# Long convolution by a two-stage transform: filters and short convolutions as two streams, filter spectra turned through DRAM, second stage without a split

## The chip, the cores and the metric

The kernel runs on one core of one Trainium2 chip. The metric is the device time of one execution in microseconds. The kernel before takes 4048.68 us (median of three runs, 4048.43 to 4051.03). The profile that is read below is one execution of 4047.38 us, of which 4045.6 us are the span from the first to the last instruction.

## What is computed

The kernel is one layer of an encoder on 2048 positions of 1024 channels. It has a projection, then two mixers side by side (a recurrent one, RWKV-7, and a long convolution, Hyena), a gated merge, and a dense feed-forward block. The change lies in the Hyena mixer, 512 channels wide:

```python
def long_conv(z, h_fwd, h_bwd, d_skip):
    L = z.shape[1]; n = 2 * L
    zf = jnp.fft.rfft(z, n=n, axis=1)
    hf = jnp.fft.rfft(h_fwd, n=n, axis=0) + jnp.conj(jnp.fft.rfft(h_bwd, n=n, axis=0))
    y = jnp.fft.irfft(zf * hf[None], n=n, axis=1)[:, :L]
    return y + z * d_skip

def hyena_mixer(u, conv_w, conv_b, ..., skip):
    u = short_conv3(u, conv_w, conv_b)            # 3 taps along the positions
    v, x1, x2 = jnp.split(u, 3, axis=-1)
    h = hyena_filters(L, ...)                     # a small network times exp(-t * delta)
    z = x1 * long_conv(v, h[:, 0, 0], h[:, 0, 1], sk[0])
    z = x2 * long_conv(z, h[:, 1, 0], h[:, 1, 1], sk[1])
    return z
```

## The kernel before

The program runs its stages one after the other: the projection (to about 650 us), the recurrent mixer (to about 1654 us, called the chain below), the Hyena mixer (1654 to about 2190 us), the merge and the feed-forward block. Only the end of the chain and the Hyena mixer are changed.

**The Hyena mixer** works on four tiles c of 128 channels (`HT` = 4). The Fourier transform of 4096 points is done as two stages of small matrix products. The first stage of a signal is `fwd` (four steps of eight 64x128x128 matmuls, then a copy from PSUM to a buffer U). Between the stages two indices, position and channel, must change places within blocks of 32: `flip` does this with four `nc.vector.transpose` of 128x1024 on VectorE (L1213), from U to a buffer V. The second stage is `step3`, one step for each of eight groups q of four 128x128 blocks.

**A product** (`product`, called twice for each c) multiplies a signal's spectrum with a filter's. For each q it does the filter's second stage (`load`: four matmuls L1267, a copy H to SBUF by ScalarE L1273, and four small DMAs that write a copy Hs with the partition blocks exchanged, L1277), the signal's second stage (`step3`), two elementwise products A and B on VectorE (L1304, L1305), and one step later the first stage of the inverse (`back`, L1289 and L1290, and a copy to Q by ScalarE L1291). `load` runs two steps ahead. For q over 0 the signal's second stage runs on a split of V in a high and a low part in fp32r: a cast on ScalarE (L197), a subtraction on VectorE (L198), and three matmuls of 512 columns (L202, L203, L204) in the place of four matmuls of 128 columns in fp32. The filter's second stage and q = 0 are in fp32. After product 1 come `inverse`, a product with x1 (L1381), `fwd` again, flips, and product 2. The result of product 2 is inverted and multiplied with x2 in `finish`, which runs inside the next c.

**The filters** come from `filt(c, o)`, a generator of 16 pieces (eight of the matmuls L1193 with the exponential window on ScalarE L1192 and the window product on VectorE L1197; eight of the matmuls L1183 with the copy L1184 to U) that ends with a flip. `pull` runs pieces between the steps of a product: in product 1 about one for each q and the rest in a burst behind it, in product 2 up to four for each q until there are none left. The pieces of the first filter begin in the last two steps of the chain and go on between the last four parts of its output (`gated`, `channel_major`), one piece behind each.

**The short convolutions** are `short(ct, byrest)`: four blocks of 512 positions, each a load from DRAM to one of two buffers cu (L1156), one ScalarE operation (L1158) and two VectorE operations (L1159, L1164). All four are written where the result is needed: x1 at the start of c, z for c+1 and x2 ahead of product 2.

**What sets the order.** TensorE's order is the order of the program text in this part (`manual_schedule`). The other engines' instructions are ordered by a scheduler that weighs program order and priorities (`high_priority(offset=FIRST)` draws an instruction forward). Each engine then works through its list in that fixed order, so an instruction that waits holds up all that stand behind it. DMAs are issued by SyncE (SP) or ScalarE (ACT), each in its own order. The PSUM pool has two buffers for each tag: `pz` (second stage), `pq`, `pf`, `po`.

## Time and profile before

| what | value |
|---|---|
| profiled execution, and its span | 4047.38 us, 4045.6 us |
| mean granted TensorE clock | 0.978 |
| TensorE busy | 3847.6 us, 95% of the span |
| VectorE busy | 2418.9 us, 60% |
| ScalarE busy | 1489.7 us, 37% |
| TensorE busy from 1700 to 2200 us, per 100 us | 88.9, 87.7, 89.3, 90.2, 82.7 us |
| VectorE busy from 1700 to 2200 us, per 100 us | 80.6, 81.6, 85.7, 78.6, 71.7 us |
| DMA share from 1700 to 2200 us | 0.20 to 0.30 |

One execution is profiled; times are microseconds unless marked ns. PE is TensorE, DVE VectorE, ACT ScalarE, SP SyncE. `L1213` is a line of the kernel before. A row of groups names line, engine, operation, output <- inputs by the program's names, the shapes and the number of instructions, then busy time and the mean of one in ns, then the idle time of the engine just before them and what ended it. A row of a timeline names start, length, and in brackets the idle time ahead with its releaser. In a table by windows PEclk is the granted TensorE clock as a share of full speed.

### The profile page before, as it was taken

The numbers are of one execution on the slowest core, as the hardware profiler recorded it, in microseconds if no ns is written. First come the engines' busy times: TensorE is split into PE (matmuls) and PEld (weight loads), VectorE is DVE, ScalarE is ACT, GpSimd is POOL, SyncE is SP. The second block draws the span as 40 slices with busy tenths as digits, with TensorE's granted clock in tenths as the row PEclk, the third lists the DMA queues.
The fourth block names the chain that finished last, engine by engine and source line by source line (L and its number), as shares of the span: only waits on it lengthen the run. The fifth ranks groups of instructions, "written<-read, shape, count | busy, mean of one in ns | idle before, by whom it ended". The sixth has DMA issues, their size and how long they took to land. (4 is left out here: it accounts for less than half of the span.)

```text
span 4045.6 us, 64349 instructions
## 1 busy us (share of the span) xinstructions
PE 3847.6 (95%) x25872; PEld 3135.6 (78%) x25872; DVE 2418.9 (60%) x3823; ACT 1489.7 (37%) x2914; POOL 76.8 (2%) x107
## 2 busy tenths in 40 slices
PE   8999999899998999788897999999999999999998
PEld 6766557777776777788887999788888878888887
DVE  4456884565666665678877655544444474444444
ACT  3345662333335565756554323211111151111113
POOL 0000000000000000000000000000000000000000
PEclk9999999999999999899999999999999999999999
DMA  4566878676677666322224434511111132111111
GB/s 137 171 169 178 216 201 240 197 211 195 207 214 206 198 188 200 91 56 69 62 74 145 151 117 126 167 52 47 47 47 47 47 116 93 47 47 47 47 47 42
DMA packets 389185, 501.83 MB, mean 124 GB/s; under 512 B 134852, under 2 KB 270541, under 8 KB 388181
## 3 DMA queue, kind: packets, MB, share of 16 engines
q1 hardware_dynamic: 362775, 443.13, 36.8%
q10 hardware_dynamic: 20736, 37.80, 3.1%
q0 software_dynamic: 5376, 16.78, 1.4%
q8 instruction: 204, 3.34, 0.4%
q14 instruction: 94, 0.77, 0.1%
HBM read 352.74 MB, written 127.93 MB: 119 GB/s over the span
## 5 line engine op out<-in xcount | busy, mean ns | idle before, releaser
L202 PE MATMUL acc<-xh,wh 128*128 128x512 f32 x1376 | 584.9, 425 | 9.2 <-ACT xh L197 9.2
L203 PE MATMUL acc<-xl,wh 128*128 128x512 f32 x1376 | 553.8, 402 | 6.9 <-DVE xl L198 6.9
L204 PE MATMUL acc<-xh,wl 128*128 128x512 f32 x1376 | 552.7, 402 | 0.5 <-DVE wl L198 0.5
L1644 DVE TENSOR_TENSOR acc<-pd,acc 128x1024 f32<-128x1024 f32 x320 | 387.8, 1222 | 68.7 <-PE pd L204 63.5
L197 ACT CAST fwh<-raw 128x1024 fp32r<-128x1024 f32 x132 | 138.5, 1049 | 703.8 <-PE pg L203 486.1
L202 PEld LDWEIGHTS acc<-xh,wh 128*128 128x128 f32 x1376 | 263.9, 192 | 125.0 <-issue 48.4
L1672 DVE TENSOR_TENSOR h<-pu,sg 128x512 f32<-128x512 f32 x88 | 60.9, 692 | 492.1 <-PE pu L204 486.1
L203 PEld LDWEIGHTS acc<-xl,wh 128*128 128x128 f32 x1376 | 265.0, 193 | 70.0 <-DVE xl L198 9.9
L204 PEld LDWEIGHTS acc<-xh,wl 128*128 128x128 f32 x1376 | 264.4, 192 | 65.6 <-DVE wl L198 1.1
L202 PE MATMUL pd<-fwh,hh 128*128 128x512 f32 x704 | 275.8, 392 | 2.1 <-DVE acc L1642 1.7
L204 PE MATMUL pu<-fxh,fwl 128*128 128x512 f32 x704 | 277.5, 394 | 0.0
L204 PE MATMUL pg<-fxh,fwl 128*128 128x512 f32 x704 | 277.1, 394 | 0.0
L203 PE MATMUL pg<-fxl,fwh 128*128 128x512 f32 x704 | 276.1, 392 | 0.0
L202 PE MATMUL pg<-fxh,fwh 128*128 128x512 f32 x704 | 275.9, 392 | 0.2 <-DVE fxl L1559 0.2
L202 PE MATMUL pu<-fxh,fwh 128*128 128x512 f32 x704 | 275.4, 391 | 0.4 <-ACT fxh L1558 0.4
L203 PE MATMUL pu<-fxl,fwh 128*128 128x512 f32 x704 | 275.8, 392 | 0.0
L203 PE MATMUL pd<-fwl,hh 128*128 128x512 f32 x704 | 275.2, 391 | 0.0
L204 PE MATMUL pd<-fwh,hl 128*128 128x512 f32 x704 | 274.2, 389 | 0.0
L198 DVE TENSOR_TENSOR fwl<-raw,fwh 128x1024 fp32r<-128x1024 f32 x132 | 161.3, 1222 | 167.0 <-ACT fwh L197 163.1
L198 DVE TENSOR_TENSOR wl<-wraw,wh 128x512 fp32r<-128x512 f32 (+1 forms) x217 | 169.3, 791 | 149.4 <-ACT wh L197 132.3
L197 ACT CAST wh<-wraw 128x512 fp32r<-128x512 f32 (+1 forms) x217 | 151.0, 705 | 290.5 <-PE acc L203 248.9
L1213 DVE STREAM_TRANSPOSE V<-U 128x1024 f32<-128x1024 f32 x96 | 181.2, 1955 | 30.3 <-ACT U L1291 12.4
(299 smaller groups left out, 7569.9 us busy)
## 6 DMA issues: line engine op xcount, KB each, us to landing
wraw<-in_w_in SPq DMA_DIRECT2D x130, 512.0 KB, 4.4
ABp<-ABd SPq DMA_DIRECT2D x64, 512.0 KB, 4.7
raw<-in_fg SPq DMA_DIRECT2D x44, 512.0 KB, 3.5
raw<-in_fu SPq DMA_DIRECT2D x44, 512.0 KB, 3.4
raw<-in_fd SPq DMA_DIRECT2D x44, 512.0 KB, 3.4
ud<-ev ACTq DMA_DIRECT2D x84, 256.0 KB, 3.4
ABd<-AB SPq DMA_DIRECT2D x32, 512.0 KB, 4.6
gated<-ev SPq DMA_DIRECT2D x64, 256.0 KB, 3.0
```

The source lines that it names most:

```text
L197: nc.scalar.copy(hi, src)
L198: nc.vector.tensor_tensor(out=lo, in0=src, in1=hi.bitcast(F32), op=ALU.subtract)
L202: mm(ps, ah, bh, start=start, stop=False)
L203: mm(ps, ah, bl, start=False, stop=False)
L204: mm(ps, al, bh, start=False, stop=stop)
L1213: self.nc.vector.transpose(V[:, :, sl].rearrange("p j c -> p c j"), U[:, :, sl].rearrange("p n c -> p c n"))
L1644: tt(out=acc[t], in0=pf, in1=acc[t], op=ALU.add)
L1672: tt(out=h, in0=put, in1=sg, op=ALU.mult)
```

## The change

Four things are rewritten together.

1. **Second stage.** `parts` and the split go, with the split constant matrix `Ms`. `step3` runs in fp32 for the signal at every q, as for the filter.
2. **Filter flips.** A filter's spectrum isn't flipped on VectorE any more. Each piece of 128x512 is copied from PSUM to one of two spots in SBUF (the free half of cu0, or ring buffer 11) and stored from there by ScalarE's DMA queue to a tensor `Hd` in DRAM; `turned_filter` loads V with four DMAs of 32 partitions on SP's queue, with the two indices exchanged. U then holds signals only.
3. **Filters as one stream.** `filters()` is one generator for all eight filters, `upto(n)` runs it to its piece n. In the last steps of the chain five pieces stand where 4.0 us of them stood, and between its last four output parts 2, 6, 1 and 0 in the place of one each. In product 1 the pieces but nine are spread over q, and nine follow in a burst. Ahead of product 2 stand four pieces, and 12 are spread over its q. The window and its product share a buffer.
4. **Short convolutions as one stream.** `shorts()` yields after each block of 512 in the order z(0), x1(0), z(1), x1(1), x2(0), z(2) and so on, and issues the load of the next block ahead of the work on this one. Four blocks are spread over the q of product 1 and eight over those of product 2 (four in the last). The first two `load` of product 1, which stood ahead of `finish`, now stand behind it.

```diff
-    def short(self, ct, byrest):
+    def shorts(self):
...
+        cts = [0, HT]
+        for c in range(HT):
+            cts += [c + 1, HT + c + 1, 2 * HT + c] if c + 1 < HT else [2 * HT + c]
+        seq = [(ct, b) for ct in cts for b in range(NB)]
...
+        u = given(0)
+        for k, (ct, b) in enumerate(seq):
+            nxt = given(k + 1) if k + 1 < len(seq) else None
...
+            u = nxt
+            yield
...
+    def filters(self):
...
+                def spec(q, g):
...
+                    u = self.spots[q % 2].rearrange("p (a b) -> p a b", b=P)
+                    nc.scalar.copy(u, p)
+                    nc.scalar.dma_start(self.Hd[c, o, 4 * q:4 * q + 4].rearrange("n p c -> p n c"), u)
...
-        self.Vfs[c, o] = self.flip(U)
+    def upto(self, n):
+        while self.pieces < n and next(self.taps, 0) is None:
+            self.pieces += 1
...
+    def turned_filter(self, c, o):
+        self.upto(32 * c + 16 * o + 16)
+        V = self.hy.tile([P, 32, P], F32, name="V", tag="post", bufs=3)
+        for k in range(4):
+            self.nc.sync.dma_start(V[32 * k:32 * k + 32], self.Hd[c, o, :, 32 * k:32 * k + 32])
+        return V
...
-            def step3(hi, lo, q):
+            def step3(v, q):
                 p = ps.tile([P, 4, P], F32, name="pz", tag="pz")
-                if lo is not None:
-                    self.mm3(p.rearrange("p a b -> p (a b)"), Mh, Ml, hi.rearrange("p a b -> p (a b)"), lo.rearrange("p a b -> p (a b)"), True, True)
-                    return p
                 for j in range(4):
-                    mm(p[:, j], Mc[:, 0 if 4 * q + j == 0 else 3], hi[:, j], start=True, stop=True)
+                    mm(p[:, j], Mc[:, 0 if 4 * q + j == 0 else 3], v[:, 4 * q + j], start=True, stop=True)
                 return p
...
-            def product(Vf, Vz, Q, fill, share, tag, hs):
-                AB = {}
-                room = s.tile([P, 16, P], F32R, name="vh", tag=tag, bufs=1)
+            def product(Vf, Vz, Q, goal, convs):
+                AB, begin = {}, self.pieces
+                hs = {q: load(Vf, q) for q in range(2)}
...
-                    pull(fill, share if q < 7 else 0.0)
+                    self.upto(begin + (goal - begin) * min(q + 1, 7) // 7)
                     if q > 0:
                         back(q - 1)
+                    for _ in range(convs * (q + 1) // 8 - convs * q // 8):
+                        next(self.conv)
...
-                for part in (gated(2), channel_major(1), channel_major(0), gated(0)):
+                for part, k in ((gated(2), 2), (channel_major(1), 6), (channel_major(0), 1), (gated(0), 0)):
                     self.pull(part, 1e9)
-                    self.pull(taps, 0.8)
-                self.taps = taps
+                    self.pull(taps(k), 1e9)
...
                 for c in range(HT):
                     x = zt("x1")
-                    moves = turned(self.short(HT + c, True), x)
-                    Vf = self.Vfs.pop((c, 0))
-                    hs = {q: load(Vf, q) for q in range(2)}
+                    moves = turned(self.short(HT + c), x)
                     if post:
                         finish(*post)
                     pull(moves, 1e9)
-                    taps = self.filt(c, 1)
-                    Q = product(Vf, Vz, self.pre(c + 1), taps, 0.8, "z", hs)
-                    pull(taps, 20.0)
+                    more, at = c + 1 < HT, 32 * c + 32
+                    Q = product(Vf, Vz, self.pre(c + 1), at - 9, 4 if more else 0)
+                    self.upto(at)
+                    Vf = self.turned_filter(c, 1)
...
-                    x2 = self.short(2 * HT + c, False)
-                    pull(taps, 1e9)
-                    taps = self.filt(c + 1, 0) if more else iter(())
-                    Vf = self.Vfs.pop((c, 1))
-                    Q = product(Vf, Vz, self.pre(c), taps, 3.0, "x1", {q: load(Vf, q) for q in range(2)})
-                    pull(taps, 1e9)
-                    post = c, Q, x2
+                    self.upto(at + 4)
+                    Q = product(Vf, Vz, self.pre(c + 1), at + 16, 8 if more else 4)
+                    post = c, Q, self.short(2 * HT + c)
                     if more:
+                        Vf = self.turned_filter(c + 1, 0)
```

The lists of two engines show where the scheduler puts this. The first place is ScalarE at the start of product 2 of the second channel tile. `pfz` is the PSUM of the forward transform, `z<-ph` the copies of the next tile's turned signal, `rg<-pz` the copies H of the filter's second stage, `pg` and `pf` a filter's two halves, `cu_16310` and `cu_16334` the two buffers of the short convolutions. The list before:

```order
L1248 COPY U<-pfz 128x4x128 x8
L1235 COPY z<-ph 128x512 x4
L1273 COPY rg<-pz 128x512 x3
L197 CAST vh<-V 128x512 x2
L1192 ACTIVATE rg<-delta,k_c_tcol 128x128 x4
L1184 COPY U<-pf 128x512
```

and the list of the change at the same place:

```order
L1278 COPY U<-pfz 128x4x128 x5
L1265 COPY z<-ph 128x512 x4
L1164 ACTIVATE co<-cu_16310,k_conv_b,k_conv_w 128x512
L1164 ACTIVATE co<-cu_16334,k_conv_b,k_conv_w 128x512
L1201 COPY cu_16310<-pf 128x512
L1211 ACTIVATE rg<-delta,k_c_tcol 128x128
L1202 DMA Hd<-cu_16310 128x4x128
L1211 ACTIVATE rg<-delta,k_c_tcol 128x128 x3
L1164 ACTIVATE co<-cu_16310,k_conv_b,k_conv_w 128x512
L1164 ACTIVATE co<-cu_16334,k_conv_b,k_conv_w 128x512
L1289 COPY rg<-pz 128x512 x3
```

The three copies H, which stood right behind the copies of z, now stand behind four blocks of a short convolution (x2), the last two of which are loaded into buffers that the first two must first give back.

The second place is VectorE from `finish` to the first steps of product 1, in the third channel tile. `co<-pv` is the product with x2 that ends `finish`, `rg<-pz` the products A and B. The list before:

```order
L1213 STREAM_TRANSPOSE V<-U 128x32x32 x8
L1330 TENSOR_TENSOR co<-pv,co 128x8x64 x2
L198 TENSOR_TENSOR vh<-V,vh 128x512 x2
L1330 TENSOR_TENSOR co<-pv,co 128x8x64 x2
L1304 TENSOR_TENSOR rg<-pz,rg 128x512
L1305 TENSOR_TENSOR rg<-pz,rg 128x512
L1197 TENSOR_TENSOR rg<-pg,rg 128x512
L1164 SCALAR_TENSOR_TENSOR co<-cu_16309,k_conv_w,cv 128x16x32
```

and the list of the change:

```order
L1244 STREAM_TRANSPOSE V<-U 128x32x32 x8
L1346 TENSOR_TENSOR co<-pv,co 128x8x64 x4
L1170 SCALAR_TENSOR_TENSOR co<-cu_16310,k_conv_w,cv 128x16x32
L1170 SCALAR_TENSOR_TENSOR co<-cu_16334,k_conv_w,cv 128x16x32
L1153 MEMSET cu_16334 128x1
L1165 SCALAR_TENSOR_TENSOR cv<-cu_16310,k_conv_w,cv 128x512
L1318 TENSOR_TENSOR rg<-pz,rg 128x512
L1170 SCALAR_TENSOR_TENSOR co<-cu_16310,k_conv_w,cv 128x16x32
L1216 TENSOR_TENSOR rg<-pg,rg 128x512
L1151 MEMSET cu_16310 128x1
L1165 SCALAR_TENSOR_TENSOR cv<-cu_16334,k_conv_w,cv 128x512
L1319 TENSOR_TENSOR rg<-pz,rg 128x512
```

The first product A (L1318) now stands behind the end of two convolution blocks and the first operation of a third, and B (L1319) behind the first operation of a fourth; in the list before no convolution stood ahead of them.

More of the change, by code (lines that the diff above doesn't have):

```diff
@@ L939, in chain, with taps @@
             more, left = columns(), [5.16 * 88]
+            def taps(k):
+                for _ in range(k):
+                    self.upto(self.pieces + 1)
+                    yield 0.87
             LAST = N - 3
@@ L1038, in chain @@
                 self.fps = ps, "pg", 3
-                taps, pieces = iter(()), [1, 2, 3]
+                self.taps, pieces = self.filters(), [1, 2, 3]
                 self.rush = 0
@@ L1099, in open @@
         self.Gc = [self.wp.tile([P, 16, 64], F32, name="Gc", tag="wl", bufs=2) for k in range(2)]
[L1100 to L1101 removed]
+        self.turns = dict(w=0, A=0, B=0, H=0, Hs=0)
+        self.smalls, self.pieces = {}, 0
+        self.spots = [cu[:, 514:1026], self.ring(11)]
         self.tcol = self.load(self.fp, "c_tcol")
@@ L1107, in open @@
         self.taken(0)
-        self.cus = [cu, self.ring(13, 514)]
-        self.z0 = self.short(0, True)
+        self.cus = [cu, self.wp.tile([P, 514], F32, name="cu1", tag="ex")]
+        self.conv, self.convs = self.shorts(), {}
+        self.z0 = self.short(0)
         for k in range(2):
@@ L1203, in filt @@
-        spec(7, last)
-        yield 0.87
-        self.Vfs[c, o] = self.flip(U)
+        for c in range(HT):
+            for o in range(2):
+                fw4, delta, skip = self.smalls.pop((c, o))
+                if (c, o) != (HT - 1, 1):
+                    self.small(c + o, 1 - o)
+                def spec(q, g):
+                    ps, tag, bufs = self.fps
+                    p = ps.tile([P, 4, P], F32, name="pf", tag=tag, bufs=bufs)
+                    for j in range(4):
+                        mm(p[:, j], self.Fc[:, 4 * q + j], g[:, j], start=True, stop=True)
+                    u = self.spots[q % 2].rearrange("p (a b) -> p a b", b=P)
+                    nc.scalar.copy(u, p)
+                    nc.scalar.dma_start(self.Hd[c, o, 4 * q:4 * q + 4].rearrange("n p c -> p n c"), u)
+                last = None
+                for q in range(8):
+                    g = self.next("w")
+                    ps, tag, bufs = self.fps
+                    p = ps.tile([P, 4, P], F32, name="pg", tag=tag, bufs=bufs)
+                    for j in range(4):
+                        n = 4 * q + j
+                        nc.scalar.activation(g[:, j], delta, AF.Exp, scale=self.tcol[:, n:n + 1])
+                        mm(p[:, j], self.H3[:, n], fw4, start=True, stop=n != 0)
+                        if n == 0:
+                            mm(p[:, j], self.e0[0:1], skip[0:1], start=False, stop=True)
+                    with self.tc.high_priority(offset=2 * FIRST):
+                        nc.vector.tensor_tensor(out=g, in0=p, in1=g, op=ALU.mult)
+                    yield
+                    if q > 0:
+                        spec(q - 1, last)
+                        yield
+                    last = g
+                spec(7, last)
+                yield
```

106 lines of the change are left out of this document (28 added, 78 removed).

## The prediction, as put on record

> **What bounds the kernel now.** I read the shares of the engines first, then windows over the stage that changes, then who TensorE waits for there, then the timeline around the longest waits.
>
> ```profile
> PE 3847.6 (95%) x25872; PEld 3135.6 (78%) x25872; DVE 2418.9 (60%) x3823; ACT 1489.7 (37%) x2914; POOL 76.8 (2%) x107
> ...
> 1900.00:2000.00 100.00, 89.25 (x777) 83.18 (x775) 85.69 (x98) 57.95 (x119) 0.00 (x0) 0.98 0.26 70
> 2100.00:2200.00 100.00, 82.71 (x704) 76.81 (x703) 71.67 (x83) 41.87 (x81) 0.00 (x0) 0.95 0.30 85
> ```
>
> In the window rows the columns are PE, PEld, DVE, ACT and POOL busy, then the granted clock and the DMA share. TensorE bounds this stage too, but VectorE is nearly as full (85.7 of 100 us). What can be won is TensorE's idle time, some 10 us in 100. The waits from 1605 to 2200 us (total, times, longest):
>
> ```profile
> PE pz L1267 <- DVE V L1213: 15.5, 5, 6.0
> PE pgt L874 <- ACT y L866: 11.2, 8, 4.4
> PE pg L1193 <- DVE rg L1197: 9.3, 10, 2.2
> PE pv L1328 <- ACT rg L1336: 8.8, 4, 2.9
> PE pfz L1246 <- DVE z L1381: 8.3, 6, 1.5
> PE pz L202 <- DVE rg L1305: 4.7, 3, 1.6
> PE pf L1183 <- ACT U L1184: 2.3, 2, 1.2
> ```
>
> Most are waits for VectorE, and short ones. No one wait is the kernel's limit: the sum of many decides, and so where the change puts work on VectorE and ScalarE counts as much as how much it takes away.
>
> **Part 1, second stage without a split.**
>
> ```profile
> 1967.91 1.06 PE L1267 MATMUL pz<-V,Mc 128*128 128x128 f32 x8
> 1968.72 0.48 PE L202 MATMUL pz<-vh,Ms 128*128 128x512 f32 x1
> 1969.04 0.40 PE L203 MATMUL pz<-vh,Ms 128*128 128x512 f32 x1
> 1969.28 0.39 PE L204 MATMUL pz<-vh,Ms 128*128 128x512 f32 x1
> 1969.51 1.05 PE L1193 MATMUL pg<-fw,H3b 128*128 128x128 f32 x8
> 1970.40 0.39 PE L1289 MATMUL pq<-rg,Mc 128*128 128x128 f32 x2
> ```
>
> From start to start, an fp32 group and a split trio take 1969.51 - 1967.91 = 1.60 us, and a fp32 group of four takes 1970.40 - 1969.51 = 0.89, so two take 1.78. Seven q in eight products make 56 trios: 56 x 0.18 = **+10** on TensorE, all on the path.
>
> What goes elsewhere:
>
> ```profile
> L1213 DVE STREAM_TRANSPOSE V<-U 128x1024 f32<-128x1024 f32 x96 | 181.2, 1955 | 30.3 <-ACT U L1291 12.4 <-ACT U L1248 10.8 <-ACT U L1184 7.0
> L198 DVE TENSOR_TENSOR vh<-V,vh 128x512 fp32r<-128x512 f32 x56 | 38.1, 686 | 0.5 <-ACT vh L197 0.5
> L197 ACT CAST vh<-V 128x512 fp32r<-128x512 f32 x56 | 33.7, 616 | 30.1 <-DVE V L1213 22.9 <-PE pz L204 6.3
> ```
>
> VectorE loses 38.1 here and ScalarE 33.7.
>
> **Part 2, filter flips through DRAM.** 32 of the 96 transposes go, a third of 181.2, or 60 us; with the subtractions VectorE has about 98 us less to do. ScalarE gets 64 issues. The nearest rows for the transfers (KB each, then us from issue to landing):
>
> ```profile
> rg<-rg SPq DMA_DIRECT2D x256, 64.0 KB, 2.0
> cu<-ud SPq DMA_DIRECT2D x22, 256.5 KB, 3.2
> ...
> yrd<-yo SPq DMA_DIRECT2D x16, 256.0 KB, 2.9
> ...
> N<-Nd POOLq DMA_DIRECT2D x8, 512.0 KB, 5.0
> ```
>
> A store of 256 KB takes 2.9, four loads of 128 KB (512 KB in all) at most 5.0: with the last copy 0.6 a filter is back about 9 after its last piece. The shortest cover is at the change of c: four forward steps of two groups of 0.89 (7.1), and in `finish` eight groups of inverse and four of transposes; with the 16 transposes of x1 that is some 14 of TensorE's work (the smaller ones counted at 0.45 a group). I cost it at nothing; if that cover were gone it would be a wait at each of eight filters (a rival below). DMA is busy only 0.26 to 0.30 of the time.
>
> With those flips out of VectorE's list, three sorts of short waits should go: pfz for z 8.3, pz for L1305 4.7, pf for U 2.3, together **-15**. The bounds are 0 and that plus the 9.3 of pg for L1197; I take the middle row because the burst of nine pieces, where pg waits, stays.
>
> **Part 3, the filter stream.** At the end of the chain:
>
> ```profile
> 1643.76 0.36 PE L1193 MATMUL pg<-fw,H3b 128*128 128x128 f32 x1
> 1648.21 0.47 PE L874 MATMUL pgt<-k_c_ident,y 128*128 128x128 f32 x1 [4.08 <-ACT y L866]
> ...
> 1649.14 1.92 PE L1183 MATMUL pf<-rg,Fc 128*128 128x128 f32 x8
> ```
>
> Six pieces of 0.89 now stand ahead of this wait and fill the 4.08 (the 4.4 of the table of waits lies earlier and stays, since no piece is put there). The piece after it ran at half pace (1.92), so another 2 comes back: **-6**, with -4 more at the start of the mixer, where the first filter's pieces no longer alternate with VectorE: **-10**, bounds 0 and -14.
>
> **Part 4, the short convolutions.** Here I expect the loss. Rows for durations:
>
> ```profile
> L1164 DVE SCALAR_TENSOR_TENSOR co<-cu,k_conv_w,cv 128x512 f32<-128x512 f32 x29 | 31.4, 1117 | 0.3
> L1158 ACT ACTIVATE co<-cu,k_conv_b,k_conv_w 128x512 f32<-128x512 f32 x16 | 13.0, 813 | 10.8 <-DMA cu<-ud 10.8
> L1164 DVE SCALAR_TENSOR_TENSOR co<-cu,k_conv_w,co 128x512 f32<-128x512 f32 x16 | 12.0, 751 | 0.4
> L1159 DVE SCALAR_TENSOR_TENSOR co<-cu,k_conv_w,co 128x512 f32<-128x512 f32 x16 | 11.9, 747 | 5.9 <-ACT co L1158 5.7
> L1304 DVE TENSOR_TENSOR rg<-pz,rg 128x512 f32<-128x512 f32 x64 | 44.0, 688 | 43.5 <-PE pz L204 34.6 <-PE pz L1267 8.8
> L1273 ACT COPY rg<-pz 128x512 f32<-128x512 f32 x64 | 37.2, 585 | 28.3 <-PE pz L1267 21.3 <-DMA rg<-rg 4.5 <-DVE rg L1304 2.4
> ...
> SPq L1156 <- DVE co L1164: 45.0, 20, 10.0
> ```
>
> The last row says that a load of cu already waits for the VectorE operation that frees its buffer (20 times). What is queued behind it is the matter.
>
> *Start of product 2.* Before:
>
> ```profile
> 2006.64 7.40 DVE L1213 STREAM_TRANSPOSE V<-U 128x1024 f32<-128x1024 f32 x4 [3.71 <-ACT U L1248]
> ...
> 2008.78 2.33 PE L1267 MATMUL pz<-V,Mc 128*128 128x128 f32 x19
> 2014.18 1.13 PE L1267 MATMUL pz<-V,Mc 128*128 128x128 f32 x8 [3.07 <-DVE V L1213]
> ```
>
> TensorE waits 3.07 for the four flips of Vz. In the change, count from F, the end of the forward transform. VectorE: three flips (1.85 each) from F+0.7 to 6.3, two filter products (0.69, as L1304) to 7.6, the fourth flip to 9.5, then block 1 of x2 (0.75 + a filter product 0.69 + 0.75) to 11.7. Only then is cu0 free; its load lands at 14.9, ScalarE works on it to 15.7; cu1 is free at 13.2, lands at 16.4, is done at 17.2. Behind these two in ScalarE's list stand the copies H, so the first is there at 17.8. TensorE: 16 transposes of z and two pieces to F+4.1, a wait for the filter product to 7.0 (2.9), a piece each of pf and pg and two filter steps to about 10.5; the third step needs a PSUM buffer that the copy H frees: wait to 17.8 (**7.3**). A further 1.1 goes to B, whose exchanged copy takes the swap's 2.0 and its issues. Together 11.3 against 3.07, or +8.2 in c = 1 and 2. In c = 0 one block stands ahead in the place of two, so about +4: **+20** in all. Bounds: if the loads were there in time only the flips' wait is left, 0; if each block cost its full load once more, 30.
>
> *Start of product 1 in c = 1, 2, 3.* Count from T, the end of x1's transposes. They free the row buffer that two waiting blocks write; VectorE ends the first at T+1.1, the load lands at 4.3, ScalarE ends at 5.1, and copy H of the third group at 5.7, where TensorE, with five groups of 0.89, stood at 4.5 (wait 1.2). VectorE's A comes after this block, at 6.5, and B after 1.12 + 0.69 + 0.75 + 0.69 more, at 9.8, against TensorE at 6.6: wait 3.2. About 4.5 each, nothing of it before: **+13**; bounds 0 and 20.
>
> *`finish`.*
>
> ```profile
> 1943.11 1.15 PE L1328 MATMUL pv<-k_c_ident,rg 128*128 128x128 f32 x8 [2.87 <-ACT rg L1336]
> 1944.09 3.60 PE L1232 MATMUL ph<-k_c_ident,co 128*128 128x128 f32 x16
> ...
> 1944.00:1948.00 4.00, 4.00 (x24) 3.64 (x23) 2.61 (x3) 2.03 (x4) 0.00 (x0) 0.57 0.15 66
> ```
>
> The two filter steps ahead of it (1.78) are moved behind it, so that much cover is gone while VectorE does the same eight flips: the wait of 2.87 becomes about 5. Three times +2.2: **+7**, bounds 0 and +9.
>
> **The clock.** After that 2.87 us wait the granted clock stood at 0.57, and 16 transposes took 3.60. The longest wait of the stage shows the same:
>
> ```profile
> 2145.60 3.64 PE L1267 MATMUL pz<-V,Mc 128*128 128x128 f32 x16 [6.00 <-DVE V L1213]
> ```
>
> Two groups that take 1.78 took 3.64, so a long wait costs 1.9 more behind it. The wait of 7.3 does so three times (5.7), the 3.2 perhaps every second time (2.8): **+9**; bounds 0 and 15. The Trainium skill, TensorE: Matmul & The Clock Gate, Part 1, has a threshold: half the clock after an idle window of about 3.4 us, with a free-running window. By that rule alone only the 7.3 would pay, and the sum would be 3 us lower; the 2.87 with its 0.57 shows that here a shorter wait can pay too.
>
> **The sum.** 10 - 15 - 10 + 20 + 13 + 7 + 9 = +34 on the profiled 4047.4, so 4081. The profiled execution lies 1.3 below the median, within the runs' spread (4048.4 to 4051.0), so I say **4082**.
>
> **The rivals.**
> *Relief wins (faster).* One mechanism: VectorE, with 98 us less, is early at the start of product 2, so that blocks 1 and 2 of x2 are done while the forward transform still runs and the loads of blocks 3 and 4 are there when ScalarE comes to them. It decides there: the second block would have to be done on VectorE by F+6.5 (TensorE's 10.5 less 3.2 of load and 0.8 of ScalarE), where I have 13.2. Then the 20, 13 and 9 fall away: 4047.4 + 34 - 42 = 4039, and with half of pz's 15.5 for V gone too, 4032. For it: VectorE is 85.7% full, and all these waits are on it. Against it: VectorE's list puts the blocks behind three or four flips, which wait for the last forward copy and cannot be early.
> *Half and half.* The loads wait, but only for one block, as in c = 0: half of 20 + 13 + 9 falls away, 4082 - 21 = 4061; with pg's 9.3 gone as well, 4052: no change.
> *The trip through DRAM is the bound.* If stores and loads, behind SP's small swaps, took twice the 9, TensorE would wait 5 and lose 1.9 in clock at the four changes of c: 4082 + 28 = 4110. Against it: DMA is busy 0.26.
>
> **How the numbers follow.** 0.51 for the forecast, 0.30 for relief, 0.12 for half and half, 0.07 for DRAM. Changes under 0.2% (8 us) can't be told from none here. Faster: 0.30; same: most of half and half and no more, 0.11; slower: the rest, 0.59. The forecast's own range is 4057 (the four losses of 20, 13, 7 and 9 at half: 4081 - 24) to 4106 (at their upper bounds 30, 20, 9 and 15: 4081 + 25). For 8 in 10 the range has to take in relief, with some more of the waits for VectorE gone: 4022 to 4106.
>
> **What would show it.** Right: a wait of 6 to 8 us of pz for the copy H at the start of product 2 in c = 1 and 2, with ScalarE idle there for a load of cu; a wait of pz for a VectorE product some 5 us into product 1; VectorE's busy time about 100 lower; no PE wait for a V that comes by DMA; the wait of 4.08 for y gone and the one of 4.4 still there. Wrong: if waits at the start of product 2 stay near 3 us, the convolution blocks were not in the way, and the time is then below 4040.

## The result, and the profile after

The changed kernel takes 4107.41 us (median of four runs, 4103.74 to 4115.43) against 4049.47 us for the kernel before in the same session (four runs, 4048.43 to 4051.03). The ratio is 1.0145, with a 95% interval of 1.0128 to 1.0163: **58 us slower**. The forecast was 4082, slower; the result is 25 us above it and 1.4 above the upper end of the range.

The profiled execution took 4106.99 us (span 4105.2, mean granted clock 0.969). The page's first part:

```profile
PE 3884.3 (95%) x26152; PEld 3176.9 (77%) x26152; DVE 2346.5 (57%) x3734; ACT 1462.0 (36%) x2857; POOL 76.8 (2%) x107
```

and the same two windows of 100 us as before (columns PE, PEld, DVE, ACT, POOL busy, granted clock, DMA share, GB/s):

```profile
1900.00:2000.00 100.00, 86.79 (x710) 83.17 (x709) 56.46 (x68) 44.99 (x94) 0.00 (x0) 0.89 0.43 111
2100.00:2200.00 100.00, 81.23 (x703) 75.68 (x703) 65.77 (x64) 42.56 (x82) 0.00 (x0) 0.90 0.46 118
```

VectorE is relieved: 56.5 us busy in a window where it had 85.7. TensorE is idle only a little more (86.8 busy, before 89.3). The number to see is the granted clock: 0.89 and 0.90, where it stood at 0.98 and 0.95.

To say how much each is worth, I cut the stage into windows of 2 us, from the same wait of the chain (`pR`, at 1606 us before) to the last inverse's wait for its flips, and added up three things. Idle is the window less TensorE's busy time; work is busy time times granted clock; clock is busy time times what is missing of the clock.

| from one profiled execution each, us | length | idle | work | clock |
|---|---|---|---|---|
| kernel before | 575.3 | 79.3 | 471.8 | 24.2 |
| changed kernel | 634.2 | 98.2 | 480.9 | 55.1 |
| difference | +58.9 | +18.9 | +9.1 | +30.9 |

All of the loss lies in this stage, and **just over half of it is the clock** (30.9 of 58.9).

The waits of TensorE from 1605 to 2260 us in the changed kernel (total, times, longest):

```profile
PE pz L1283 <- ACT rg L1289: 27.4, 16, 5.8
PE pf L1199 <- DVE rg L1216: 15.5, 8, 2.9
PE po L1335 <- DVE V L1244: 9.8, 4, 3.7
PE pv L1344 <- DVE co L1346: 6.8, 6, 2.8
PE pz L1283 <- DMA V<-Hd: 6.8, 1, 6.8
PE pgt L875 <- ACT y L867: 6.7, 4, 5.7
PE ph L1262 <- ACT z L1265: 5.6, 4, 4.9
PE pg L1212 <- DVE rg L1216: 5.5, 5, 1.5
PE pf L1199 <- ACT rg L1201: 3.5, 1, 3.5
...
PE pfz L1276 <- DVE z L1392: 0.3, 1, 0.3
```

The longest group is new: pz waits for ScalarE's copy H (L1289). The waits of pfz for z, 8.3 before, are nearly gone. The start of product 2 in the third tile, on TensorE:

```profile
2048.09 2.08 PE L1199 MATMUL pf<-rg,Fc 128*128 128x128 f32 x8 [2.86 <-DVE rg L1216]
...
2051.43 1.95 PE L1283 MATMUL pz<-V,Mc 128*128 128x128 f32 x16
2059.18 3.78 PE L1283 MATMUL pz<-V,Mc 128*128 128x128 f32 x16 [5.80 <-ACT rg L1289]
```

and on ScalarE at the same time:

```profile
2055.98 0.81 ACT L1164 ACTIVATE co<-cu,k_conv_b,k_conv_w 128x512 f32<-128x512 f32 x1 [3.76 <-DMA cu<-ud]
2057.84 0.81 ACT L1164 ACTIVATE co<-cu,k_conv_b,k_conv_w 128x512 f32<-128x512 f32 x1 [1.05 <-DMA cu<-ud]
2058.56 1.05 ACT L1289 COPY rg<-pz 128x512 f32<-128x512 f32 x2
```

The copy H that TensorE waits for stands behind two convolution operations, and ScalarE sits idle for the load of each. TensorE's rows show what the wait does besides: sixteen matmuls of the filter's second stage take 1.95 ahead of it and 3.78 behind it.

`finish` in the same tile, on TensorE:

```profile
1960.11 3.68 PE L1335 MATMUL po<-V,Gc 128*64 128x128 f32 x32 [2.02 <-DVE V L1244]
...
1969.53 0.63 PE L1344 MATMUL pv<-k_c_ident,rg 128*128 128x128 f32 x4 [1.56 <-DVE co L1346]
```

and in windows of 3 us around the first of these waits:

```profile
1956.00:1959.00 3.00, 1.97 (x19) 1.59 (x17) 3.00 (x2) 2.03 (x4) 0.00 (x0) 1.00 0.84 169
1959.00:1962.00 3.00, 1.89 (x18) 1.89 (x20) 3.00 (x3) 0.00 (x0) 0.00 (x0) 0.50 0.03 5
1962.00:1965.00 3.00, 3.00 (x24) 2.34 (x22) 3.00 (x3) 1.17 (x2) 0.00 (x0) 0.50 0.00 0
```

A wait of 2.02 us, and the clock is at 0.50 for the next five.

The filters' way through DRAM, by the DMA issues of that window (KB each, median us to landing):

```profile
V<-Hd SPq DMA_DIRECT2D x32, 512.0 KB, 7.8
...
Hd<-cu ACTq DMA_DIRECT2D x32, 256.0 KB, 2.5
Hd<-rg ACTq DMA_DIRECT2D x32, 256.0 KB, 2.6
```

The loads of V are 512 KB each, four to a filter, not the 128 KB that I had read into them, and land after 7.8 us, not 5.0 at most. In the changed kernel that is seen once, in the last tile:

```profile
2195.17 7.66 PE L1283 MATMUL pz<-V,Mc 128*128 128x128 f32 x40 [6.80 <-DMA V<-Hd]
```

### The profile page after: what moved, and what is told of

Read it like the earlier page. It is cut to its first block, busy times and chain, and to the rows that moved or that the text cites. A ratio compares the mean times of both kernels' runs of the same rounds, so it can differ in the third digit from the quotient of the medians.

```text
span 4105.2 us, 64939 instructions
## 1 busy us (share of the span) xinstructions
PE 3884.3 (95%) x26152; PEld 3176.9 (77%) x26152; DVE 2346.5 (57%) x3734; ACT 1462.0 (36%) x2857; POOL 76.8 (2%) x107
## 3 DMA queue, kind: packets, MB, share of 16 engines
q1 hardware_dynamic: 364311, 459.91, 38.4%
## 5 line engine op out<-in xcount | busy, mean ns | idle before, releaser
L1283 PE MATMUL pz<-V,Mc 128*128 128x128 f32 x1024 | 142.9, 296 | 36.5 <-ACT rg L1289 27.4
```

What stands on the lines that cost most here:

```text
L1283: mm(p[:, j], Mc[:, 0 if 4 * q + j == 0 else 3], v[:, 4 * q + j], start=True, stop=True)
```

## The experiments

All ratios are to the kernel before on the same chip, where it took 4033 to 4038 us, with 95% intervals. One execution of each was profiled; it lies up to 18 us from the median of its runs, so differences of a few us in the stage are read only where a named wait shows them. Idle, work and clock are those of the stage as above. The theory is that of the prediction: the convolution's loads in ScalarE's list make the loss. Its rivals: TensorE's extra work, the trip through DRAM, and, once the result was seen, the clock.

**The change once more.**

> The change itself, beside the same runs of the kernel before as the three that follow, whose ratios are to be read against this one. All theories: a ratio of 1.013 to 1.0165.

1.0153 (1.0125 to 1.018). The stage has idle 101.4, work 481.1, clock 58.2: the same picture on another chip.

### One part alone

**Second stage unsplit, in the kernel before.**

```diff
-                if q == 0:
-                    return v, None
+                return v, None
...
```

> The kernel before with the second stage unsplit for the signal, and nothing else. Theory 'order': +10 us of TensorE work, less up to 10 us of waits for VectorE and ScalarE that have 38 and 34 us less to do: 4049 to 4062. Theory 'split': 4080 or more. 'DRAM': as 'order'.

1.0038 (1.0022 to 1.0054), +15 us. In the stage work is up 13, clock 10, idle down 2.6. VectorE and ScalarE lose 38 and 34 us of operations, and TensorE's idle time hardly moves. The term of +10 for TensorE's work held (9.1 in the change itself); that less work on VectorE gave so little idle time back is a first sign against the -15, though that term was for the flips.

**Filter flips through DRAM, in the kernel before** (stored from U, loads where the flip stood).

```diff
+            nc.scalar.dma_start(self.Hd[c, o, 4 * q:4 * q + 4].rearrange("n p c -> p n c"), U[:, 4 * q:4 * q + 4])
...
-        self.Vfs[c, o] = self.flip(U)
+        V = self.hy.tile([P, 32, P], F32, name="V", tag="post", bufs=3)
+        for k in range(4):
+            nc.sync.dma_start(V[32 * k:32 * k + 32], self.Hd[c, o, :, 32 * k:32 * k + 32])
+        self.Vfs[c, o] = V
```

> The kernel before with the filters' flips replaced by the trip through DRAM (store from U on ScalarE's queue, four loads on SP's), and nothing else. VectorE loses 60 us of flips. Theory 'order': waits for VectorE shrink by 5 to 15 us, 4034 to 4050. Theory 'DRAM': 4080 or more, with TensorE waiting for V that comes by DMA.

1.0109 (1.007 to 1.0149). Work 471.2, as before; idle 103.4 and clock 39.0. Its waits:

```profile
PE pz L1272 <- DMA V<-Hd: 23.3, 5, 9.0
PE pq L1295 <- DVE rg L1310: 19.8, 3, 6.8
PE pz L1272 <- ACT rg L1278: 18.3, 4, 6.5
```

The second row is not a VectorE wait at its root. Product B needs the swapped copy Hs, and SyncE issued its swaps behind the loads of V, on the same queue, and VectorE waits for them:

```profile
1766.64 2.63 SPq L1209 DMA_DIRECT2D V<-Hd  x4
1769.37 2.41 SPq L1282 DMA_DIRECT2D rg<-rg  x4
...
1779.95 0.69 DVE L1310 TENSOR_TENSOR rg<-pz,rg 128x512 f32<-128x512 f32 x1 [6.86 <-DMA rg<-rg]
```

The queue held the swaps up by the 2.6 us of these issues. The longer part of the wait is their landing: all were issued by 1771.8, and the last of them came at 1779.95, just behind the last load of V (1779.14), where a swap lands after 2.0 us in the kernel before. So the trip costs on its own, wherever nothing long enough stands in front of it. The changed kernel escapes these waits by putting the filter's first steps behind `finish`.

**The change with the split put back** in the signal's second stage.

```diff
...
-                    p = step3(Vz, q)
+                    p = step3(Vz, q, zs)
+                    if q < 7:
+                        zs = parts(Vz, q + 1, room)
...
```

> The change with the split second stage of the kernel before, and nothing else undone. If the unsplit stage costs its TensorE work alone: 10 us less than the change, ratio 1.012 to 1.0135. If it costs the 15 to 20 us that it cost alone on the kernel before: 1.0095 to 1.0115. If the casts and subtractions come in the way of the streams: 1.015 or more.

1.018 (1.0159 to 1.0201), not faster than the change. TensorE's work falls to 471.4 as it should, but idle rises to 112.6: the waits of pz for ScalarE's copy H grow from 27.4 to 29.1 + 7.3. The profiled execution is the slowest of its four, 15 us above their median, so these sizes are rough. They fit the third expectation, that the casts and subtractions push the copies back further; no row here singles it out.

### One placement undone

**The two first filter steps ahead of `finish` again.**

```diff
...
                     moves = turned(self.short(HT + c), x)
+                    hs = {q: load(Vf, q) for q in range(2)}
                     if post:
                         finish(*post)
...
```

> The change with the first two filter steps of product 1 ahead of finish, as before. Theory 'order': the waits of 2.0 us for the flip and of 1.4 to 2.8 us for the product with x2 shrink by some 2 us each time and the clock stays up behind them: 3 x (2 + 3) = 15 us at most, ratio 1.0105 to 1.013. Rival (the flips of VectorE set that wait, whatever stands ahead): 1.014 to 1.016.

1.0131 (1.0105 to 1.0157). The waits in `finish` fall from 9.8 to 3.7 for V and from 6.8 to 0.4 for the product with x2 that its transposes wait for, and those for the copy H fall from 27.4 to 19.0. Waits for V from DRAM come instead: 13.7 (2.6, 2.7 and 8.4; a fourth of 2.5 is put down to nothing), where the change has 6.8. Much of what `finish` gives comes back as the trip.

**The convolutions where they were**, all four blocks written where the result is needed; the load of the next block is still issued one block ahead.

```diff
-            cts += [c + 1, HT + c + 1, 2 * HT + c] if c + 1 < HT else [2 * HT + c]
+            cts += [c + 1, 2 * HT + c, HT + c + 1] if c + 1 < HT else [2 * HT + c]
...
-                    Q = product(Vf, Vz, self.pre(c + 1), at - 9, 4 if more else 0)
+                    Q = product(Vf, Vz, self.pre(c + 1), at - 9, 0)
...
+                    x2 = self.short(2 * HT + c)
                     self.upto(at + 4)
-                    Q = product(Vf, Vz, self.pre(c + 1), at + 16, 8 if more else 4)
-                    post = c, Q, self.short(2 * HT + c)
+                    Q = product(Vf, Vz, self.pre(c + 1), at + 16, 0)
+                    post = c, Q, x2
```

> The change with the short convolutions in the order and at the places of the kernel before (x2 whole ahead of product 2, none inside the products). Theory 'order': the waits of pz for the copy H at the start of product 2 (27 us in all) mostly go, with the clock behind them: 4107 - 20 to 35, ratio 1.006 to 1.0105. Rival (the blocks have to be done somewhere, and VectorE does them later in the way of something else): 1.0125 or more.

1.0131 (1.0108 to 1.0155), some 6 to 9 us less than the two runs of the change, whose intervals overlap with it. It doesn't take the wait at product 2 away:

```profile
PE pz L1283 <- ACT rg L1289: 22.1, 13, 4.5
PE pg L1212 <- DVE rg L1216: 11.2, 6, 3.5
PE pv L1344 <- DVE co L1346: 10.3, 5, 4.2
```

ScalarE at the start of product 2 in the third tile:

```profile
2041.65 0.81 ACT L1164 ACTIVATE cv<-cu,k_conv_b,k_conv_w 128x512 f32<-128x512 f32 x1 [3.39 <-DMA cu<-ud]
...
2043.76 1.05 ACT L1289 COPY rg<-pz 128x512 f32<-128x512 f32 x2
```

In the place of x2's last blocks, blocks of another convolution (by the text's order, x1 of the next tile) now stand ahead of the copies H and wait for their loads, and TensorE waits 4.50, 3.39 and 4.16 at the three starts. The waits of pg and pv grow. So it does not matter which convolution stands there; what hurts is that an operation that waits for a load stands ahead of the copies.

**The chain's end as before**, one piece between each of its last four parts.

```diff
-                for part, k in ((gated(2), 2), (channel_major(1), 6), (channel_major(0), 1), (gated(0), 0)):
+                for part, k in ((gated(2), 1), (channel_major(1), 1), (channel_major(0), 1), (gated(0), 1)):
```

> The change with one piece of the filters between the last parts of the chain's output, as before, in the place of 2, 6, 1 and 0; the rest of the first filter follows behind. Theory 'order': the pieces wait for each other's window products and spots there (3.5 us for a spot, then 4.9 us for z behind them) and gain nothing; without them 0 to 10 us come back. Rival (they fill the wait of 4 us for y, as I forecast): 4 to 10 us more.

1.0158 (1.0133 to 1.0182), the same as the change. Waits of 1.48 (pg), 3.75 (pgt for y) and 2.77 (pz for V from DRAM) stand in the place of 3.52 (pf for the first spot's copy) and 4.89 (ph for z).

### The order of the lists

**ScalarE in the order of the text**, as TensorE.

```diff
-            with tc.manual_schedule(engines={mybir.EngineType.PE}):
+            with tc.manual_schedule(engines={mybir.EngineType.PE, mybir.EngineType.Activation}):
```

> The change, with ScalarE's list in the order of the program text in the Hyena mixer (TensorE's is so already). The copies H then stand ahead of the short convolution's blocks at the start of product 2. Theory 'order' (the loss is made by waiting blocks of the short convolution in front of what TensorE needs, and by the clock that falls after each such wait): the waits of pz for the copy H of 3.5, 4.5 and 5.8 us go, and with each about 2 us of half clock: 4107 - 20, so 4080 to 4095. Theory 'split' (the unsplit second stage costs more than its 10 us) and theory 'DRAM' (the trip of the filters costs it): within 4 us of 4107.

The theory's strongest test: no work, no transfer and no place in TensorE's list changes, only the order of ScalarE's list, and with it what stands ahead of the copies H.

```profile
PE pfz L1276 <- ACT U L1278: 9.0, 2, 8.7
PE pr L203 <- DVE y L198: 7.8, 1, 7.8
...
PE pz L1283 <- ACT rg L1289: 6.1, 5, 2.5
...
PE pr L202 <- DVE rs L1453: 5.2, 1, 5.2
```

The waits for H fall from 27.4 to 6.1, and the stage up to the merge (its first matmul pr) from 624.5 to 599.2, where the kernel before has 566.7. Idle time falls by 8 of these 25 us (94.5 to 86.2) and the clock's loss by 18 (54.6 to 36.4): the order of ScalarE's list cost more in clock than in waiting. The time is 1.0133 (1.0101 to 1.0165) all the same, which can't be told from the change's 1.0145 and 1.0153. Text order is wrong at the two ends: a forward transform at the start waits 8.7 for a copy of U, and the merge behind the mixer waits 7.8 and 5.2.

**VectorE in the order of the text too.**

> As before, with VectorE's list in the order of the program text too: no block of a short convolution stands ahead of the products A and B any more; the fourth flip goes ahead of the window products. Theory 'order': the waits of 2.2 us at the start of product 1 go as well, 4070 to 4090. 'split' and 'DRAM': within 4 us of 4107.

1.0179 (1.0144 to 1.0214). One row has grown from 15.5:

```profile
PE pf L1199 <- DVE rg L1216: 40.7, 7, 6.7
```

In this order the window products stand behind all four flips of a signal.

### The clock

**Redundant matmuls where TensorE waits**, in the change (three groups ahead of the first pf of the four pieces at product 2, four to six behind its second filter step, two in `finish`) and in the kernel before (three groups ahead of the flipped steps, three among the transposes of `finish`). Their results are overwritten by the matmuls behind them, or are the same once more.

```diff
+            def warm(p, n):
+                for k in range(4 * n):
+                    mm(p[:, k % 4], Mc[:, 3], Mc[:, 3], start=True, stop=True)
...
```

> The change with redundant fp32 matmuls, whose results are overwritten or are the same, put where TensorE waits: three groups of four ahead of the first pf at the start of product 2, four or six ahead of its third filter step, two ahead of the inverse in finish. Some 11 groups or 10 us of added work for each channel tile, none of it needed. Theory 'idle clock' (the clock halves after waits of about 2 us and more, and 31 of the 59 us lost are that): the waits are filled, the clock stays up, and the time falls by 12 to 25 us, a ratio of 1.008 to 1.0115 to the kernel before. Theory 'load clock' (the clock falls because of the heavier fp32 work, not because of idling): no fall, or a rise by up to 20 us, 1.0145 to 1.020.

> The kernel before with redundant matmuls in its two long waits of each channel tile (three groups ahead of the signal's first step of product 2, six in the last; three ahead of the second transpose of finish). Theory 'idle clock': of 10 us lost to the clock between the first product 2 and the last inverse, 5 to 10 come back, ratio 0.9972 to 0.9990. Theory 'load clock': 1.000 to 1.003.

| us in the stage | idle | work | clock |
|---|---|---|---|
| change, its second run | 101.4 | 481.1 | 58.2 |
| change with redundant matmuls | 88.5 | 510.8 | 37.2 |
| before | 79.3 | 471.8 | 24.2 |
| before with redundant matmuls | 65.0 | 495.2 | 17.5 |

The clock comes back in both: 21 us of it against 30 of added work in the change, 7 against 23 before. So it is the waiting that takes the clock, and not more matmuls. No time comes of it: 1.0181 (1.0157 to 1.0206) and 1.0005 (0.9991 to 1.002). In the kernel before the stage even became 2 us longer: gaps that end when another engine's work ends are filled, but not shortened. The added work was also more than the waits took in: 30 us of it replaced 13 of idle time in the change, and 23 replaced 14 before. A smaller dose was not tried.

### Putting the better halves together

**Loads ahead of `finish`, one piece between the chain's parts, ScalarE in text order in the first three tiles only**; and the same with the split.

```diff
...
-                for c in range(HT):
+            for c in range(HT):
+                hand = {mybir.EngineType.PE, mybir.EngineType.Activation} if c + 1 < HT else {mybir.EngineType.PE}
+                with tc.manual_schedule(engines=hand):
...
```

> The change with three of its orders put right together: the first two filter steps of product 1 ahead of finish, one piece between the chain's last parts, and ScalarE in the order of the program text inside the first three channel tiles (copies H ahead of the short convolution; the end is left to the scheduler). Theory 'order': most of the loss is order, and with it put right 25 to 45 us come back: ratio 1.0035 to 1.0085. Rival (each cure only moves the wait to the next VectorE product): ratio 1.010 or more.

> The same three orders with the split second stage of the kernel before, so that the streams and the trip through DRAM are what is left of the change. TensorE has 10 us less work, VectorE 38 and ScalarE 34 more. If the unsplit stage costs only its TensorE work: 10 us below the run without the split. If it costs the 15 to 20 us that it cost alone, and VectorE's relief of 60 us is then worth something: at or below the kernel before, ratio 0.995 to 1.002. If the casts and subtractions come in the way: above the run without the split.

1.0103 (1.0075 to 1.0132) and **1.0069 (1.0045 to 1.0094)**, the best of all. The waits for H are gone from the first rows, and one stands in their place (each kernel has its row):

```profile
PE pz L1283 <- DMA V<-Hd: 26.6, 5, 6.4
```

```profile
PE pz L1296 <- DMA V<-Hd: 25.8, 5, 6.6
```

The trip is now in the open. In mix_split the last store of a filter was issued at 1772.9, the loads at 1777.7 to 1779.5, and TensorE went on at 1791.6: 19 us, where I had said 9.

The kernel of the second of these (mix_split) was executed once more, unchanged, on the chip of the next two versions.

> One look more at the run with the three orders put right and the split second stage, beside the two that follow: within 8 us of its 4064, with four waits of about 6 us for the filter from DRAM.

4071.83 us in this one execution, some 8 us more than there, with idle 88.8 and clock 38.4 against 87.1 and 35.9.

**Product 2's pieces over five q in the place of seven**, so that a filter ends two steps earlier, with the split and without (`n` is 5 in product 2 and 7 in product 1).

```diff
-                    self.upto(begin + (goal - begin) * min(q + 1, 7) // 7)
+                    self.upto(begin + (goal - begin) * min(q + 1, n) // n)
```

> The same kernel with the 12 pieces inside product 2 spread over its first five q in the place of seven, so that each filter starts its trip through DRAM some 10 us earlier. If the trip is the cause of what was left: the waits for the filter of about 6 us in c = 1, 2, 3 go and with them 15 to 25 us, ratio 1.000 to 1.003. If something else takes their place (the flips of Q, the product with x2): less than 8 us gained, ratio 1.005 or more.

> The same without the split. If the trip is the cause of what was left: 15 to 25 us below the 4079 of the mixed unsplit kernel, ratio 1.004 to 1.007. Its distance to the run with the split gives the price of the unsplit stage once more: 10 us by its work.

1.0112 (1.0095 to 1.0129) and 1.0099 (1.0083 to 1.0114). With the split, V is waited for 18.8 in the place of 25.8, but the denser pieces make new waits (pfz for U 7.5). Without it the waits for V did not shrink at all (28.2), though the stores were earlier. ScalarE and SyncE say why:

```profile
1771.44 0.37 ACTq L1202 DMA_DIRECT2D Hd<-rg  x1
...
1776.96 6.12 SPq L1154 DMA_DIRECT2D cu<-ud  x3
1783.17 2.00 SPq L1235 DMA_DIRECT2D V<-Hd  x4
...
1797.02 3.75 PE L1283 MATMUL pz<-V,Mc 128*128 128x128 f32 x16 [6.59 <-DMA V<-Hd]
```

The last store went at 1771.44, and the loads of V stood on SyncE's queue until 1783.17, behind loads of cu that wait for their buffers. A late convolution holds up the filter. The price of the unsplit stage, 15 us alone and 15 between the two mixed versions, does not show here: the version without the split is 10 us shorter than the one with it (4073.76 and 4083.26, with intervals that overlap).

**The loads of V on a queue of their own** (GpSimd's), with pieces over five q and without the split, and then on mix_split.

```diff
-            self.nc.sync.dma_start(V[32 * k:32 * k + 32], self.Hd[c, o, :, 32 * k:32 * k + 32])
+            self.nc.gpsimd.dma_start(V[32 * k:32 * k + 32], self.Hd[c, o, :, 32 * k:32 * k + 32])
```

> The run with the orders put right, unsplit, the pieces of product 2 in its first five q, with the four loads of each filter issued by GpSimd in the place of SyncE. Theory 'SyncE's queue': the loads start 8 us earlier, the waits of 6.5 us for the filter in c = 1, 2, 3 go, and 15 to 30 us with them: ratio 1.002 to 1.006 (from 1.0099). Theory 'the trip itself': the waits stay above 4 us, ratio 1.008 or more.

> The run with the orders put right and the split, pieces of product 2 over seven q, filter loads issued by GpSimd. There SyncE issued the loads only some 2 us after the last store had landed, so little is to be gained from the queue: both theories say that a wait of 4 to 6 us for the filter stays; ratio 1.005 to 1.008 (from 1.0069).

1.0172 (1.0147 to 1.0198) and 1.0082 (1.0051 to 1.0113). In the second the waits for V fall from 25.8 to 18.7. In the first they fall to one of 5.4, and a larger one comes:

```profile
PE pfz L1276 <- ACT U L1278: 30.2, 4, 11.2
```

ScalarE at one of these waits:

```profile
2081.52 0.81 ACT L1164 ACTIVATE co<-cu,k_conv_b,k_conv_w 128x512 f32<-128x512 f32 x1 [9.67 <-DMA cu<-ud]
2082.24 0.56 ACT L1308 COPY U<-pq 128x512 f32<-128x512 f32 x1
2082.70 0.58 ACT L1278 COPY U<-pfz 128x512 f32<-128x512 f32 x1
```

and the landing times of the loads of cu:

```profile
DMA to landing us min/median/max: 2.9/3.5/12.6
```

While the 2 MB of a filter move, a load of 256 KB that lands in 3.5 us takes up to 12.6, and ScalarE waits 9.67 for it with the copies of U behind it. That load was issued at 2068.91, 1 us behind the filter's last, and landed at 2081.49, 0.2 us behind it. So the order of the queue was one part of the delay, and the transfers themselves are another.

No version beat the kernel before. Text order on ScalarE in three tiles, without the other edits, was not tried.

## Why the prediction was right or wrong

**The direction and the cause of the new wait: right.** ScalarE idles 3.76 and 1.05 us for loads of cu with the copies H behind them, TensorE waits 5.80 in the third tile and 4.46 in the second (7.3 was forecast, and 6 to 8 named as the sign), and the reordering of ScalarE's list alone takes 21 us of the waits for H away.

**The step that failed is the clock.** It was priced at +9, for the wait of 7.3 three times and for the 3.2 every second time; it measured **+30.9**. The half-clock row of 2.87 was in the prediction, and I let only two kinds of new wait pay; the 2.9 for the window product, which my own count of the start of product 2 had, was left without a price, and it came in the first three tiles (2.83, 2.86 and 2.86). From all 236 waits of TensorE of at least 0.9 us in 13 of the 20 profiles (1650 to 2200 us, clock at full for the 4 us before), with "halved" for a granted clock of 0.70 or less in the 2.5 us behind:

| length of the wait, us | waits | halved |
|---|---|---|
| 0.9 to 1.5 | 60 | 2 |
| 1.5 to 1.8 | 42 | 8 |
| 1.8 to 2.7 | 58 | 37 |
| 2.7 to 3.2 | 41 | 31 |
| over 3.2 | 35 | 34 |

The half clock then mostly stays for 3 to 7 us. The clock records of all 20 traces know only full and half, and each stretch of half lasts 3.41 us or a whole multiple of it (the last one of each trace is cut off by its end). From 1650 us to the last inverse 9 such stretches begin in the kernel before, 38 us in all, and 18 in the change, 109 us in all. The table misses those that begin later: behind each of the three waits of 3.06 to 3.07 in the kernel before the clock halves 1.7 to 1.9 us on, and they count as not halved. In a cycle of the change (1898 to 2048 us) five waits paid (2.86, 4.46, 2.02, 2.20 + 0.94, and 1.92 + 1.14), in a cycle before two. What counts is how many waits are over about 2 us, more than how much waiting there is: idle time rose by a quarter, the clock's loss more than twofold. The Trainium skill, TensorE: Matmul & The Clock Gate, Part 1, gives an idle window of about 3.4 us for this. The stretches of 3.41 us agree with the length of that window, but a wait need not be as long: here two thirds of the waits of 1.8 to 2.7 us already halve the clock, and the measurement decides.

**The idle time came near by terms that offset each other.** Forecast +15, measured +18.9:

| term | forecast | measured |
|---|---|---|
| relief of VectorE (all other places) | -15 | -11.4 |
| end of the chain, start of the mixer | -10 | +3.8 |
| start of product 2 | +20 | +15.7 |
| start of product 1 | +13 | +7.6 |
| `finish` | +7 | +3.2 |

The measured column adds up waits of 0.5 us and more at each place. The last tile adds 1.9 (0.8 at product 2, where it waits 6.80 for V from DRAM and before 6.00 for flips, and 1.1 at the last inverse), and the waits under 0.5 us take 1.9 back. The *relief*: the three sorts of waits that I named are gone at these places, all 15.3 us of them, but waits for the window products grew by 3.3 and those for the filter's copies by 2.1. The *chain* was wrong in sign: the 4.08 for y is gone as forecast, but the 4.43 became 5.72, pf waits 3.52 for the copy that frees the first spot, and ph 4.89 for z. *Product 1* waits for ScalarE's copy H only, not for VectorE's product B, which I had put at 3.2:

```profile
1980.77 1.16 PE L1283 MATMUL pz<-V,Mc 128*128 128x128 f32 x8 [2.20 <-ACT rg L1289]
1982.87 2.08 PE L1283 MATMUL pz<-V,Mc 128*128 128x128 f32 x8 [0.94 <-ACT rg L1289]
```

**TensorE's work**: +10 forecast, +9.1 measured.

**The relief was smaller than counted.** VectorE has 72 us less, not about 98. Each flip that is left takes longer:

```profile
L1244 DVE STREAM_TRANSPOSE V<-U 128x1024 f32<-128x1024 f32 x64 | 137.3, 2210 | 31.3 <-ACT U L1278 17.7 <-ACT U L1308 13.6
```

2210 ns against 1955 before, for the same shape: 64 x 0.255 = 16 of the missing 26 us; the other 10 are not traced. Eight in a row take 16.84 where they took 14.79, about as much as the wait of 2.02 in `finish`.

**The trip through DRAM**: the sizes were misread by a factor of four (512 KB a load, not 128) and the time to landing with them. I forecast no wait for it, and there is only the one of 6.80: the first two `load` of product 1 stand behind `finish`. As a cause it is hidden and not absent: it came out at 14 to 28 us of waits for V in the versions in which they stand ahead of `finish` and SyncE issues the filter's loads.

**The rivals.** Relief wins: no, the second block of x2 was not in time (VectorE ends it in the third tile some 14 us after the forward transform, and by F + 6.5 it would have had to). Half and half: no, there are waits for H at product 2 in all three tiles (3.47, 4.46 and 5.80). What stays open is how the 43 us that the second stage does not explain divide between the clock and the waits that set it off. Filling the waits returned the clock but no time.

## What to carry to other kernels

Before an instruction that waits for a load is placed in an in-order list, look at what stands behind it for TensorE, and then at the queue that issues the load: it has the same order problem. Count TensorE's waits over about 2 us and price each with its own length and 1.7 or 3.4 us of lost clock behind it (half of 3.41 or 6.83). Work taken off an engine that is not the last to be waited for is worth little (VectorE from 86 to 56% busy in one window of 100 us, and 11 us of idle time less in all), while the transfers that replace it need cover and slow the other loads.

## What the runs showed of the hardware that was not expected

- Waits as short as 1.8 to 2.7 us were followed by half clock in 37 of 58 cases, and half clock came in stretches of 3.41 us and whole multiples of it.
- Four loads that turn 2 MB in pieces of 512 bytes landed after 7.6 to 10.9 us in the median on SyncE's queue, and a load of 256 KB beside them after 12.6 us, where the median is 3.5 and the longest in the kernel before 7.1.
- The same 128x1024 transposes took 1.94 to 1.96 us in the kernel before and in the two kernels made from it by one part, and 2.19 to 2.23 us in the change and the versions made from it, while the other VectorE operations kept their times (the product of 128x512: 688 and 690 ns). All the latter have ring tiles of 512 columns in the place of 514, which can move the buffers that lie behind them; whether that is the cause was not tried and stays open.
